# Later sums of weights, carries ahead of weight copies, and last-layer output tiles by ScalarE copy and accumulating DMA, in a two-layer hybrid trunk

## The chip, the cores and the metric

The kernel runs on one core of one Trainium2 chip. The metric is the device time of one execution in microseconds (us). A core has TensorE (PE, matrix products), VectorE (DVE), ScalarE (ACT), GpSimd (POOL) and SyncE (SP). In this kernel SP does nothing but issue DMAs, and POOL and ACT issue some too. All matrix products land in PSUM and have to be evacuated from there by DVE or ACT.

## The reference, cut to what matters

The model is a trunk of two layers over 16 meta tokens and 512 tokens, 1024 channels, float32.

```
for l in range(DEPTH):                                   # DEPTH = 2
    h = rmsnorm(h_res, norm_gain[l])
    proj = h @ w_in[l]
    u_pool, z_pool, c_q, c_kv, k_rope, z_mla, g_pool, g_mla = jnp.split(proj, IN_SPLIT_POINTS, axis=-1)
    y_pool = (pool_mix(u_pool, pool_w_group[l], pool_scale[l]) * silu(z_pool)) @ pool_w_up[l]
    o_mla = mla(c_q, c_kv, k_rope, pos, ...)             # 8 heads, causal attention
    y_mla = (o_mla * silu(z_mla)) @ mla_w_up[l]
    merged = sigmoid(g_pool) * y_pool + sigmoid(g_mla) * y_mla
    h_res = h_res + merged @ w_out[l]
return h_res[:, N_META:]
```

Two places of it matter here: `pool_w_group` (in the kernel `wgr`, the weights of the grouped pooling), and the last line of a layer, the product with `w_out` that is added to the residual stream.

## The kernel before, in words

Everything is kept with channels on the 128 partitions and tokens along the free dimension: the residual stream is `xb`, 8 tiles of 528 tokens (the last layer works on 512). A product in float32 accuracy is made of three faster ones: each operand is split into a high and a low part, and `mm3` issues high by high, low by high and high by low (L192, L195, L196). A weight tile of 128 by 512 goes through four hands: SP loads it into one of three `raw` buffers (L115), ACT copies it to the high part `whi` (L187), DVE subtracts to get the low part `wlo` (L188), and PE uses both.

`register` writes a plan, a list of products in the order in which their weights come: c_kv, c_q, then for m = 0 to 3 a pool product `u`m followed by a key product `k`m, then the values `v`, then `yw` (the load of `wgr`, `held` in two `sv` buffers until the pooling product `y` uses it), and so on to the output products. `stream` walks over the plan, calls the weight load of a product a few products ahead, and advances a clock `clk` by what it has issued. The order of the instructions on each engine is then settled by a scheduler with a simulated timeline, so a small edit can move rows on all engines. `behind(a, b)` ties instruction a behind instruction b; `newest[0]` is the newest matmul at that point, and `earlier(ns)` is the newest matmul that was issued at least so many ns ago by that clock.

The output product. Tiles o0, o1, o2 and o3 are plain products with four rows of weight chunks (evacuated by `ev_o`, L1092: one DVE instruction that adds half of the PSUM bank to `xb`). The other four tiles are made of two pairs u = 0, 1 by a scheme with seven products in place of eight (`out_pairs`): p = 1, 2, 7, 6, 5 between o2 and o3 (called "oa"), and p = 4, 3 after o3 ("ob"). It needs sums of weight tiles (`wsum`), which are made in DRAM during the layer by SP copies and accumulating POOL DMAs (`weight_sums`, L359). Bank "a" of a pair carries a running sum through the products 1, 6, 5 and 3. After p = 1, 6 and 5 its value also has to be added to another part of `xb`: `carry` (L1163) lets ACT copy the bank into an `sv` buffer, and POOL issues a DMA that adds that buffer to `xb` (L1164). The next product into the same bank can't start before the ACT copy has read it. Finished parts of `xb` leave in the last layer by `yT` DMAs (L1101 in `out`, issued by POOL, in "ob" by SP).

A row name such as `p2u1` below is product 2 of pair 1.

Of the kernel before, what the change touches and what calls it, by code (L numbers as in the profile page):

```python
# [10 lines left out]
F32R = mybir.dt.float32r  # L11
BF16 = mybir.dt.bfloat16
I32 = mybir.dt.int32
AF = mybir.ActivationFunctionType
ALU = mybir.AluOpType
# [7 lines left out]
NM = 16  # L23
# [49 lines left out]
def trunk(ctx, tc, xT, pos, win, wkr, wqb, wkb, wvb, wgr, wpu, wmu, wout, gains, const, yT):  # L73
    nc = tc.nc
    pe, act, dve, gp, sp = nc.tensor, nc.scalar, nc.vector, nc.gpsimd, nc.sync
# [11 lines left out]
    def nm(s):  # L87
        uid[0] += 1
        return f"{s}_{uid[0]}"

    def slot(tag, dt=F32, bufs=1, w=W):
        return sl.tile([P, w], dt, tag=tag, name=nm(tag), bufs=bufs)

    def tmp(w=W):
        return tp.tile([P, w], F32, tag="tmp", name=nm("tmp"), bufs=3)
# [18 lines left out]
    def fetch(src, n, raw, eng):  # L114
        eng.dma_start(raw[:, :n], src)  # L115
        return raw

    def rawt():
        return wp.tile([P, 512], F32, tag="raw", name=nm("raw"), bufs=3)
# [49 lines left out]
            return self.src[c // 512] if isinstance(self.src, list) else self.src[:, c:c + n]  # L169

    loads = [0]

    def wload(src, n, gain, spare, buf=None, held=False):
        raw = early.pop(0) if early else fetch(src, n, buf or rawt(), sp)
        loads[0] += 1
        pool, th, tl, nb = (tp, "th", "tl", 2) if loads[0] <= 2 or spare else (wp, "whi", "wlo", 3)
        if gain is not None:
            v = raw[:, :n].rearrange("p (k m) -> p k m", k=8)
            gp.tensor_mul(v, v, gain.unsqueeze(2).to_broadcast([P, 8, n // 8]))
            return raw, None  # L180
        if held:
            hi, lo = slot("sv", F32R, bufs=2), slot("sv", F32R, bufs=2)
            split(hi, lo, raw[:, :n], 0, n)
            return hi, lo
        hi = pool.tile([P, W if pool is tp else 512], F32R, tag=th, name=nm("whi"), bufs=nb)
        lo = pool.tile([P, W if pool is tp else 512], F32R, tag=tl, name=nm("wlo"), bufs=nb)
        act.activation(hi[:, :n], raw[:, :n], AF.Copy)  # L187
        dve.tensor_sub(lo[:, :n], raw[:, :n], hi[:, :n].bitcast(F32))  # L188
        return hi, lo

# [10 lines left out]
    def earlier(ns):  # L201
        return next((m for c, m in reversed(past) if c <= clk[0] - ns), past[0][1])

    newest = [None]
    plan = []
# [96 lines left out]
    def split(hi, lo, src, a, b):  # L302
        act.activation(hi[:, a:b], src, AF.Copy)  # L303
        dve.tensor_sub(lo[:, a:b], src, hi[:, a:b].bitcast(F32))  # L304

    def behind(ins, other):
        tc.add_manual_dep(ins.ins, other.ins.name,
                          mybir.DependencyInfo(mybir.DependencyClass.Sync, mybir.DependencyReason.DATA))
# [38 lines left out]
    def weight_sums(name, w):  # L347
        def made(u, i):
            a, b = w[2 * u], w[2 * u + 1]
            d = wsum[name][u]  # L350
            src = {0: (b[:, 0:512], b[:, 512:1024]), 2: (a[:, 0:512], b[:, 0:512]), 1: (a[:, 0:512], d[:, 0, :]),
                   3: (a[:, 512:1024], d[:, 1, :])}
            return d[:, i, :], src[i]

        def copy(d, src):
            behind(sp.dma_start(d, src[0]), earlier(14000))

        def add(d, src):
            behind(gp.dma_start(d, src[1], accum_op=ALU.add), earlier(4000))  # L359

        for u in range(len(w) // 2):
            for fn, i in ((copy, 0), (copy, 2), (add, 0), (copy, 1), (add, 2), (add, 1), (copy, 3), (add, 3)):
                yield lambda fn=fn, u=u, i=i: fn(*made(u, i))

    class Layer:
# [723 lines left out]
        def ev_o(self, m, nxt):  # L1089
            def ev(ps, a, b):  # L1090
                x = xb[:, m, a:b]
                dve.scalar_tensor_tensor(out=x, in0=ps, scalar=0.5, in1=x, op0=ALU.mult, op1=ALU.add)  # L1092
                self.out(m, (a, b), nxt, gp)
                if not self.last and m == 3 and b == T:
                    nxt.square_x(m)
            return ev
# [46 lines left out]
        def out_pairs(self, nxt, name, products):  # L1143
            order = [(p, u) for p in products for u in range(2)]
            l = self.l
            a, b, c = self.halves()
            n = b - a
            A, B = (a, b), (b, c)
            src = []
            for p, u in order:  # L1150
                w0, w1 = wout[l, OUT[2 * u]], wout[l, OUT[2 * u + 1]]
                src.append({1: w0[:, 0:512], 2: w0[:, 512:1024], 4: w1[:, 512:1024]}.get(p))
                if src[-1] is None:
                    src[-1] = wsum[l][u][:, {5: 0, 6: 1, 7: 2, 3: 3}[p], :]
            bank = self.banks

            def grow(m, s, v):
                x = xb[:, m, s[0]:s[1]]
                dve.scalar_tensor_tensor(out=x, in0=v, scalar=0.5, in1=x, op0=ALU.mult, op1=ALU.add)

            def carry(m, s, v, u, scale, o):
                t = self.carried[u][:, o:o + n]
                act.activation(t, v, AF.Copy, scale=scale)  # L1163
                gp.dma_start(xb[:, m, s[0]:s[1]], t, accum_op=ALU.add)  # L1164

            def body(i, w):
                p, u = order[i]
                m0, m1 = OUT[2 * u:2 * u + 2]
                key = {2: "e", 7: "c", 4: "c"}.get(p, "a"), u
                if key not in bank:  # L1170
                    bank[key] = (sct if key[0] == "a" else mmt)()
                ps = bank[key][:, :n]
                t, o = (B if p == 3 else A), (0 if p == 1 else 4)
                for k in range(4):
                    xh, xl = (x[:, t[0]:t[1]] for x in self.mg[k + o]) if p < 4 else self.tt[k][p]
                    c_ = P * k
                    mm3(ps, w[0][:, c_:c_ + P], w[1][:, c_:c_ + P], xh, xl, k == 0 and p in (1, 2, 7), k == 3, True)
                    if k == 1:
                        yield 6 * (n / 2.4)
                q = sp if name == "ob" else gp  # L1180
                if p == 1:
                    self.carried[u] = slot("sv", bufs=2)
                    carry(m0, A, ps, u, 0.5, 0)
                elif p == 2:
                    grow(m0, A, ps)
                    self.out(m0, A, nxt, q)
                elif p == 7:
                    grow(m1, B, ps)
                elif p == 6:
                    carry(m1, A, ps, u, -0.5, HALF)  # L1190
                elif p == 5:
                    carry(m1, B, ps, u, -0.5, 0)
                    self.out(m1, B, nxt, q)
                    if u == 1 and not self.last:
                        for m in range(3):
                            nxt.square_x(m)
                elif p == 4:
                    grow(m1, A, ps)
                    self.out(m1, A, nxt, q)
                else:  # L1200
                    grow(m0, B, ps)
                    self.out(m0, B, nxt, q)
                    if not self.last:
                        nxt.square_x(m0)
                        nxt.square_x(m1)
                if i == len(order) - 1:
                    done.add((l, name))
                yield 6 * (n / 2.4)

            plan.append(Gemm((l, name), src, 512 * len(src), body=body))  # L1210
            plan[-1].more = True

        def register(self, nxt):
            l, XS = self.l, self.XS
# [3 lines left out]
            def add(name, src, width, **kw):  # L1218
                plan.append(Gemm((l, name), src, width, **kw))
# [8 lines left out]
            def kk(p):  # L1228
                add(f"k{p}", wkb[l, p], 256, evac=self.ev_k(p), xs=cs, segs=FULL)
# [2 lines left out]
                cq(m)  # L1232
            for m in range(4):
                add(f"u{m}", wi(MT_U + m), D, evac=self.ev_u(m), xs=hs, segs=FULL)
                if m == 1:
                    add("kr", wkr[l], 256, body=self.kr_body, gain=gn[:, l * N_GAIN + G_H:l * N_GAIN + G_H + 8])
                kk(m)
# [4 lines left out]
                add(f"y{m}", None, P, body=self.y_body(m))  # L1242

            add("v", wvb[l], 1024, body=self.v_body)
            add("yw", wgr[l], 512, body=self.hold)
            plan[-1].held = True
            zp(0)
            zp(1)
            y(0)
# [15 lines left out]
            if self.last:  # L1265
                for e in ("gm0", "gm1", "gp0", "gm2", "gp1", "gm3", "gp2", "gm4", "gp3", "gm5", "gm6", "gm7"):
                    m = int(e[2])
# [10 lines left out]
                add(f"mu{m}", wmu[l, m], 512, evac=self.ev_mu(m), xs=lambda: self.ogs, segs=XS)  # L1278
                plan[-1].spare = m % 2 == 1
            mg = lambda: self.mg  # L1280
            self.banks, self.carried = {}, {}
            for m in range(4):
                if m == 3:
                    self.out_pairs(nxt, "oa", (1, 2, 7, 6, 5))
# [165 lines left out]
```

## Time and profile before

| | |
|---|---|
| time, median of 3 runs | 781.85 us (781.79 to 782.32) |
| the profiled execution, its own time | 781.9 us |
| its span in the trace | 780.1 us |
| granted TensorE clock | 1.00 |
| busy in the span: PE, DVE, ACT, POOL | 773.2, 569.7, 444.7, 232.7 us |
| matmuls in the trace | 5469 |
| DMA, mean over the span | 145 GB/s |

The page of the profile lists busy times by engine, the chain of work that ended last and groups of instructions by line. The timeline of one engine lists its instructions in a stretch, with the idle time before each in brackets and the instruction that ended it. Matmuls are pipelined: a row's duration (0.28 us for 256 or 264 columns) is longer than the distance between the starts of two of them (0.12 us), so a wait of PE is read as the distance between two starts less the usual distance.

### The profile page before, as it was taken

How to read it: one execution, taken by the hardware profiler on the slowest of the kernel's cores; microseconds unless marked ns; L12 is line 12 of the kernel's file. 1: busy time of each engine (PE TensorE's matmuls, PEld its weight loads, DVE VectorE, ACT ScalarE, POOL GpSimd, SP SyncE). 2: the span in 40 equal slices, each digit the busy share in tenths (PEclk: the TensorE clock that was granted, in tenths of full speed). 3: DMA queues.
4: the chain of work that ended last, by engine and by line, in shares of the span. 5: the costliest groups of instructions: out<-in, count | busy, mean ns of one | idle time of the engine just before them, and what ended most of it. 6: DMA issues, size and time to landing. Idle time of an engine off the chain costs nothing.

```text
span 780.1 us, 15325 instructions
## 1 busy us (share of the span) xinstructions
PE 773.2 (99%) x5469; PEld 710.9 (91%) x5469; DVE 569.7 (73%) x1326; ACT 444.7 (57%) x1016; POOL 232.7 (30%) x303
## 2 busy tenths in 40 slices
PE   9999999999999999999999999999999999999998
PEld 8999899999999999999997898887788999988887
DVE  5848787446778876589764577866897888864994
ACT  7645555645566665645564446546657766664552
POOL 1024525103335333211330136221006625340213
PEclk9999999999999999999999999999999999999999
DMA  6232457765646465565662424425557666662645
GB/s 245 82 96 89 125 171 151 177 168 144 156 110 164 116 141 120 156 156 184 169 171 82 109 75 122 133 62 178 146 132 167 173 187 158 175 226 72 210 137 154
DMA packets 65325, 112.92 MB, mean 145 GB/s; under 512 B 10704, under 2 KB 15696, under 8 KB 65248
## 3 DMA queue, kind: packets, MB, share of 16 engines
q1 hardware_dynamic: 55344, 92.18, 39.1%
q0 software_dynamic: 8896, 17.92, 12.9%
q10 hardware_dynamic: 1008, 1.84, 0.7%
q8 instruction: 43, 0.70, 0.4%
q14 instruction: 34, 0.28, 0.1%
HBM read 100.18 MB, written 22.62 MB: 157 GB/s over the span
## 4 chain that ended last, share of the span: by engine, by line
PE 91%; DVE 4%; DMA 2%; ACT 1%; issue 1%; POOL 0%; DVEq 0%; ACTq 0%; POOLq 0%
PE mm L192 26%; PE mm L196 26%; PE mm L195 25%; PE S L195 3%; PE S L196 3%; PE S L192 3%; PE mm L979 2%; DVE wlo L188 1%; PE o L985 1%; PE o L984 1%; PE S L506 1%; DMA raw<-wgr 1%; DMA xb<-xT 1%; PE mm L408 1%; ACT whi L187 0%
## 5 line engine op out<-in xcount | busy, mean ns | idle before, releaser
L192 PE MATMUL mm<-hh,whi 128*128 128x264 f32 (+2 forms) x992 | 306.2, 311 | 0.5 <-DVE u L550 0.4
L196 PE MATMUL mm<-hh,wlo 128*128 128x264 f32 (+2 forms) x992 | 304.4, 309 | 0.1
L195 PE MATMUL mm<-hl,whi 128*128 128x264 f32 (+2 forms) x992 | 304.1, 308 | 0.0
L188 DVE TENSOR_TENSOR wlo<-raw,whi 128x512 fp32r<-128x512 f32 (+1 forms) x253 | 180.0, 714 | 100.3 <-ACT whi L187 98.0
L187 ACT ACTIVATE whi<-raw 128x512 fp32r<-128x512 f32 (+1 forms) x253 | 154.2, 613 | 168.7 <-PE mm L195 110.2
L192 PEld LDWEIGHTS mm<-hh,whi 128*128 128x128 f32 x992 | 186.2, 188 | 11.3 <-issue 1.0
L195 PEld LDWEIGHTS mm<-hl,whi 128*128 128x128 f32 x992 | 186.8, 188 | 8.7
L196 PEld LDWEIGHTS mm<-hh,wlo 128*128 128x128 f32 x992 | 185.9, 188 | 9.0 <-DVE wlo L188 0.6
L922 POOL TENSOR_SCALAR pa<-pa,rs 128x272 f32<-128x272 f32 (+1 forms) x32 | 33.2, 1038 | 103.3 <-DVE rs L941 64.5
L922 POOL TENSOR_SCALAR cq<-cq,rs 128x400 f32<-128x400 f32 (+1 forms) x32 | 51.2, 1600 | 0.0
L192 PE MATMUL mm<-cq,whi 128*128 128x264 f32 (+2 forms) x140 | 43.8, 313 | 0.0
L195 PE MATMUL mm<-cq,whi 128*128 128x264 f32 (+2 forms) x140 | 43.7, 312 | 0.0
L196 PE MATMUL mm<-cq,wlo 128*128 128x264 f32 (+2 forms) x140 | 43.3, 312 | 0.1
L908 DVE CUSTOM_DVE_ANT_0 S<-S,maskw,nqs 128x272 f32<-128x272 f32 (+4 forms) x80 | 38.6, 498 | 5.3 <-PE S L196 5.0
L725 POOL TENSOR_TENSOR racc<-racc,tmp 128x264 f32<-128x264 f32 (+1 forms) x15 | 14.0, 936 | 85.5 <-ACT tmp L724 85.5
L304 DVE TENSOR_TENSOR tl<-mm,th 128x512 fp32r<-128x512 f32 (+1 forms) x64 | 30.0, 483 | 8.0 <-ACT th L303 6.3
L359 POOL DMA_DIRECT2D wsum<-wout x8 | 7.0, 875 | 91.6 <-PE mm L196 86.9
L303 ACT ACTIVATE th<-mm 128x512 fp32r<-128x512 f32 (+1 forms) x64 | 26.3, 433 | 10.2 <-PE mm L979 9.6
L915 ACT ACTIVATE cq<-S,bia 128x400 f32<-128x400 f32 (+2 forms) x48 | 24.5, 514 | 13.2 <-DVE bia L953 8.5
L192 PE MATMUL mm<-u,whi 128*128 128x264 f32 (+1 forms) x96 | 31.3, 326 | 0.0
L196 PE MATMUL mm<-u,wlo 128*128 128x264 f32 (+1 forms) x96 | 30.9, 322 | 0.0
L195 PE MATMUL mm<-kn,whi 128*128 128x264 f32 (+1 forms) x96 | 30.6, 320 | 0.0
(344 smaller groups left out, 1684.7 us busy)
## 6 DMA issues: line engine op xcount, KB each, us to landing
raw<-win SPq DMA_DIRECT2D x139, 256.0 KB, 2.8
raw<-wout SPq DMA_DIRECT2D x22, 256.0 KB, 3.6
bc<-kdr SPq DMA_DIRECT2D x16, 264.0 KB, 4.5
wsum<-wout SPq DMA_DIRECT2D x16, 256.0 KB, 3.5
raw<-wpu SPq DMA_DIRECT2D x16, 256.0 KB, 2.7
wsumgp<-win SPq DMA_DIRECT2D x16, 256.0 KB, 3.4
raw<-wmu SPq DMA_DIRECT2D x16, 256.0 KB, 2.8
raw<-wsumgp SPq DMA_DIRECT2D x16, 256.0 KB, 4.3
```

The costliest lines, as they stand in the source:

```text
L187: act.activation(hi[:, :n], raw[:, :n], AF.Copy)
L188: dve.tensor_sub(lo[:, :n], raw[:, :n], hi[:, :n].bitcast(F32))
L192: first = pe.matmul(out, wh, xh, start=start, stop=False, skip_group_check=more)
L195: pe.matmul(out, wh, xl, start=False, stop=False, skip_group_check=more)
L196: newest[0] = pe.matmul(out, wl, xh, start=False, stop=stop, skip_group_check=more)
L303: act.activation(hi[:, a:b], src, AF.Copy)
L304: dve.tensor_sub(lo[:, a:b], src, hi[:, a:b].bitcast(F32))
L725: self.acc_last = gp.tensor_add(self.acc[:, a:b], self.acc[:, a:b], t[:, :b - a])
L908: dve.tensor_tensor_reduce(out=sv, in0=sv, in1=mask, scale=nqs[:, i, h:h + 1], scalar=3e38, op0=ALU.add, op1=ALU.min, accum_out=bia[:, c:c ...
L915: act.activation(pv, sv, AF.Exp, scale=-1.0, bias=bia[:, i:i + 1], accum_out=rs[:, c:c + 1])
L922: gp.tensor_scalar(pt[i], pt[i], rs[:, i:i + 1], None, op0=ALU.mult)
L979: pe.transpose(tr[:, P * (i - j):P * (i - j + 1)], pt[i][:, NM + P * j:NM + P * (j + 1)], ident)
```

## The change

Five edits, in one diff:

1. `add` in `weight_sums`: the accumulating POOL DMAs are tied to a matmul 9000 ns back by the planner's clock where it was 4000.
2. `yw`: the load of `wgr` moves in the plan from behind `v` to behind `u2`; it gets a buffer of its own (tag `bc`, which the kernel otherwise uses later for another purpose) in place of one of the three `raw`, and its DMA is tied behind the newest matmul.
3. `urgent`: of the weight copies that are called for after a carry, the second and the third are tied behind the carry's ACT copy.
4. `ev_o` in the last layer, m = 0, 1, 2: ACT copies half of the bank into `tmp`, and a POOL DMA adds that to `xb`, in place of the DVE instruction.
5. The `yT` DMAs of those three tiles aren't issued by POOL at once, but by SP at the first product of "ob", behind its last matmul.

```diff
+    urgent = []
     def wload(src, n, gain, spare, buf=None, held=False):
+        if held:
+            hi, lo = slot("sv", F32R, bufs=2), slot("sv", F32R, bufs=2)
+            raw = slot("bc", bufs=3)
+            behind(sp.dma_start(raw[:, :n], src), newest[0])
+            split(hi, lo, raw[:, :n], 0, n)
+            return hi, lo
         raw = early.pop(0) if early else fetch(src, n, buf or rawt(), sp)
...
-        if held:
-            hi, lo = slot("sv", F32R, bufs=2), slot("sv", F32R, bufs=2)
-            split(hi, lo, raw[:, :n], 0, n)
-            return hi, lo
...
-        act.activation(hi[:, :n], raw[:, :n], AF.Copy)
+        made = act.activation(hi[:, :n], raw[:, :n], AF.Copy)
+        for e in urgent:
+            e[1] += 1
+            if 1 < e[1] < 4:
+                behind(made, e[0])
...
         def add(d, src):
-            behind(gp.dma_start(d, src[1], accum_op=ALU.add), earlier(4000))
+            behind(gp.dma_start(d, src[1], accum_op=ALU.add), earlier(9000))
...
             def ev(ps, a, b):
                 x = xb[:, m, a:b]
+                if self.last and m < 3:
+                    t = tmp()[:, a:b]
+                    act.activation(t, ps, AF.Copy, scale=0.5)
+                    gp.dma_start(x, t, accum_op=ALU.add)
+                    self.later.append(lambda: behind(sp.dma_start(yT[:, m, a - NM:b - NM], x), newest[0]))
+                    return
...
             def carry(m, s, v, u, scale, o):
                 t = self.carried[u][:, o:o + n]
-                act.activation(t, v, AF.Copy, scale=scale)
+                urgent.append([act.activation(t, v, AF.Copy, scale=scale), 0])
                 gp.dma_start(xb[:, m, s[0]:s[1]], t, accum_op=ALU.add)
...
+                while self.later and name == "ob":
+                    self.later.pop(0)()
...
                 add(f"u{m}", wi(MT_U + m), D, evac=self.ev_u(m), xs=hs, segs=FULL)
+                if m == 2:
+                    add("yw", wgr[l], 512, body=self.hold)
+                    plan[-1].held = True
...
             add("v", wvb[l], 1024, body=self.v_body)
-            add("yw", wgr[l], 512, body=self.hold)
-            plan[-1].held = True
```

In the changed kernel the lines lie lower: L187 is L190, L188 is L195, L303 and L304 are L310 and L311, L396 is L403, L550 is L557, L1163 is L1176, and the new ACT copy of `ev_o` is L1101.

What this does to the order of instructions is shown at three places. The first is ACT in the last layer, where the products 1 of both pairs end. `whi` rows are weight copies, `sv` rows the two carries, `sq` and `rinv` rows the splitting of other operands. Before:

```order
907 L187 ACTIVATE whi_10084<-raw_10082 128x512
908 L303 ACTIVATE sq_9831<-cq_1871_9599 128x256
909 L187 ACTIVATE whi_10105<-kh_10103 128x512
910 L187 ACTIVATE whi_10145<-kl_10143 128x512
911 L303 ACTIVATE sq_9835<-cq_1872_9601 128x256
912 L303 ACTIVATE sq_9839<-cq_1856_9557 128x256
913 L187 ACTIVATE whi_10125<-raw_10123 128x512
914 L1163 ACTIVATE sv_10036<-S_10023 128x256
915 L1163 ACTIVATE sv_10058<-S_10045 128x256
916 L303 ACTIVATE rinv_9843<-cq_1876_9627 128x256
```

The same place now:

```order
907 L310 ACTIVATE sq_9835<-cq_1872_9601 128x256
908 L310 ACTIVATE sq_9839<-cq_1856_9557 128x256
909 L1101 ACTIVATE tmp_10017<-mm_9974 128x512
910 L310 ACTIVATE rinv_9843<-cq_1876_9627 128x256
911 L1176 ACTIVATE sv_10039<-S_10026 128x256
912 L1176 ACTIVATE sv_10061<-S_10048 128x256
913 L190 ACTIVATE whi_10066<-kl_10064 128x512
914 L190 ACTIVATE whi_10087<-raw_10085 128x512
915 L190 ACTIVATE whi_10108<-kh_10106 128x512
916 L190 ACTIVATE whi_10128<-raw_10126 128x512
```

The weight copies of p7u0, p7u1, p6u1 and p6u0 stood directly ahead of the two carries, and that of p2u1 (`whi_10063`) still further up, at row 885. Now those of p2u1, p7u0, p7u1 and p6u0 (`whi_10066` to `whi_10128`; the numbers are counted anew) all stand behind them.

The second place is ACT where the same products of the first layer end. The three L396 rows (L403 now) square `xb` for the next layer's norm. Before:

```order
461 L187 ACTIVATE whi_5549<-kh_5547 128x512
462 L396 ACTIVATE cq_1005_5669<-xb 128x528
463 L396 ACTIVATE cq_1006_5671<-xb 128x528
464 L187 ACTIVATE whi_5569<-raw_5567 128x512
465 L1163 ACTIVATE sv_5480<-S_5467 128x264
466 L1163 ACTIVATE sv_5502<-S_5489 128x264
467 L396 ACTIVATE cq_1007_5673<-xb 128x528
468 L187 ACTIVATE whi_5609<-raw_5607 128x512
469 L187 ACTIVATE whi_5589<-kl_5587 128x512
```

The same place now:

```order
458 L403 ACTIVATE cq_1005_5669<-xb 128x528
459 L403 ACTIVATE cq_1006_5671<-xb 128x528
460 L403 ACTIVATE cq_1007_5673<-xb 128x528
461 L1176 ACTIVATE sv_5480<-S_5467 128x264
462 L1176 ACTIVATE sv_5502<-S_5489 128x264
463 L190 ACTIVATE whi_5507<-kl_5505 128x512
464 L190 ACTIVATE whi_5528<-raw_5526 128x512
465 L190 ACTIVATE whi_5549<-kh_5547 128x512
466 L190 ACTIVATE whi_5569<-raw_5567 128x512
```

`whi_5507` (p2u1) was row 437 before, and `whi_5528` (p7u0) was row 459; both stand behind the two carries now.

The third place is DVE in the first layer around the split of `wgr` (`sv` by L304, L311 now) and the two evacuations of u3 (the last two L550 rows, L557 now). Before:

```order
113 L539 STREAM_SHUFFLE tmp_1040<-kn_164_975 128x264
114 L188 TENSOR_TENSOR wlo_1175<-raw_1172,whi_1174 128x256
115 L540 TENSOR_TENSOR tmp_1040<-tmp_1040,ts_104 128x264
116 L188 TENSOR_TENSOR wlo_1215<-raw_1212,whi_1214 128x512
117 L550 TENSOR_TENSOR u_206_1190<-mm_1146,rinv_480 128x264
118 L304 TENSOR_TENSOR sv_1258<-raw_1255,sv_1257 128x512
119 L550 TENSOR_TENSOR u_206_1190<-mm_1147,rinv_480 128x264
```

The same place now:

```order
113 L311 TENSOR_TENSOR sv_1078<-bc_1079,sv_1077 128x512
114 L546 STREAM_SHUFFLE tmp_1040<-kn_164_975 128x264
115 L195 TENSOR_TENSOR wlo_1181<-raw_1178,whi_1180 128x256
116 L547 TENSOR_TENSOR tmp_1040<-tmp_1040,ts_104 128x264
117 L195 TENSOR_TENSOR wlo_1221<-raw_1218,whi_1220 128x512
118 L557 TENSOR_TENSOR u_209_1196<-mm_1152,rinv_480 128x264
119 L557 TENSOR_TENSOR u_209_1196<-mm_1153,rinv_480 128x264
```

The split of `wgr` went from between the two evacuations to a place five rows ahead of the first. On SP its load went from behind the two loads of `wvb` to ahead of them.

2 lines of the change are left out of this document (1 added, 1 removed).

## The prediction

> **What bounds the kernel now.** I read the page first: busy times and the chain that ended last.
>
> ```profile
> PE 773.2 (99%) x5469; PEld 710.9 (91%) x5469; DVE 569.7 (73%) x1326; ACT 444.7 (57%) x1016; POOL 232.7 (30%) x303
> PE 91%; DVE 4%; DMA 2%; ACT 1%; issue 1%; POOL 0%; DVEq 0%; ACTq 0%; POOLq 0%
> ```
>
> PE is busy in 99% of the span, and the change takes no product away. So it can only win the moments in which PE waits, and the table of PE's waits says how few those are.
>
> ```profile
> PE S L192 <- ACT sv L1163: 1.1, 1, 1.1
> PE mm L192 <- DVE u L550: 0.8, 2, 0.4
> ```
>
> The first is one wait for a carry, the second two waits for the evacuation of u3, one in each layer. Their price is the distance of two starts. First u3 in layer 0, then in layer 1 (timeline of PE):
>
> ```profile
> 83.58 0.40 PE L196 MATMUL mm<-whi,kl 128*128 128x512 f32 x1
> 84.38 0.50 PE L192 MATMUL mm<-whi,kh 128*128 128x512 f32 x1 [0.41 <-DVE u L550]
> 84.72 0.39 PE L195 MATMUL mm<-wlo,kh 128*128 128x512 f32 x1
> 84.95 0.39 PE L196 MATMUL mm<-whi,kl 128*128 128x512 f32 x1
> ```
> ```profile
> 476.03 0.40 PE L196 MATMUL mm<-whi,kl 128*128 128x512 f32 x1
> 476.48 0.50 PE L192 MATMUL mm<-whi,kh 128*128 128x512 f32 x1
> ```
>
> A 512-column matmul starts 0.23 us after the last (84.72 to 84.95). So layer 0 lost 0.80 - 0.23 = 0.57 us, layer 1 lost 0.45 - 0.23 = 0.22. After each wait the next start is also about 0.1 late (84.38 to 84.72 is 0.34); I leave that out for waits lost and waits made alike. Now the carry in the last layer, PE and then ACT:
>
> ```profile
> 755.73 0.28 PE L196 MATMUL mm<-hh,wlo 128*128 128x256 f32 x1
> 757.08 0.39 PE L192 MATMUL S<-cq,whi 128*128 128x256 f32 x1 [1.07 <-ACT sv L1163]
> ```
> ```profile
> 756.12 0.63 ACT L187 ACTIVATE whi<-raw 128x512 fp32r<-128x512 f32 x1 [1.57 <-PE mm L196]
> 756.66 0.64 ACT L1163 ACTIVATE sv<-S 128x256 f32<-128x256 f32 x2
> ```
>
> That is 1.35 - 0.12 = 1.23 us. A weight copy that waited for PE to free its buffer stood on ACT ahead of the carry that PE needed. All that the change can win is 0.57 + 0.22 + 1.23 = 2.02 us, 0.26% of 781.9. The rest of the span is PE in an even step, and ahead of it a start-up that the change leaves alone.
>
> **The early load of `wgr`.** Why u3 was late (chain of waits, layer 0):
>
> ```profile
> 79.42 2.87 DMA raw<-wgr
> 82.32 0.64 ACT sv L303
> 82.98 0.04 DVE sv L304
> ...
> 83.91 0.43 DVE u L550
> ```
>
> The load could start only when a `raw` buffer came free, at 79.42. DVE stood still for its split, between the two evacuations of u3. Now the load is tied to a matmul in the middle of u2. From 68.40, where u2 starts, 36 of its 48 matmuls at 0.121 us end near 73.0. With the same 2.87 us it lands at 75.9, and with ACT's 0.64 its high part is there at 76.6, when DVE reaches its new place only at 78.4, behind the key product's evacuation.
>
> ```profile
> 68.40 0.36 PE L192 MATMUL mm<-hh,whi 128*128 128x264 f32 x1
> 78.08 0.42 DVE L749 TENSOR_TENSOR kn<-mm,q 128x264 f32<-128x264 f32 x1
> 80.22 1.57 DVE L188 TENSOR_TENSOR wlo<-raw,whi 128x512 fp32r<-128x512 f32 x1
> 81.72 0.42 DVE L550 TENSOR_TENSOR u<-mm,rinv 128x264 f32<-128x264 f32 x1
> ```
>
> The split puts 0.6 us ahead of what stands there. The first evacuation goes from 81.72 to 82.3, the second follows at 82.7 and is over at 83.1. PE wants the banks at 83.1 and 83.8, so the whole 0.57 goes, and 0.22 in layer 1, where the order is the same. I take 0.79 won, with 0 as the other end: DVE's instructions here vary (the `wlo` at 80.22 took 1.57), and 0.5 more would give the wait back. On ACT the new copy holds up the key norms behind it until about 76.6; their first user on DVE stands behind the split, at 79.0, which covers it. On SP the load now stands ahead of both `wvb` loads, so these wait for 73.0 too; they need `raw` buffers that DVE frees with `wlo` rows later than that, so I price it at 0.
>
> **The later sums.** POOL's longest wait in sum stands in front of these DMAs:
>
> ```profile
> POOL wsum L359 <- PE mm L196: 107.6, 11, 46.9
> ```
>
> An older matmul shortens these waits and moves POOL's pooled-mean work by a row or two. Nothing in PE's waits names POOL. I take 0, from -0.1 to 0.1: sums come so early that even a wait of 46.9 on POOL held nobody up. If that cover were gone, the price would be a late weight load, as the 0.57 above.
>
> **The carries go first, layer 0.** Here PE had no wait. ACT, then PE:
>
> ```profile
> 377.47 1.16 ACT L396 ACTIVATE cq<-xb 128x528 f32<-128x528 f32 x2
> 378.75 0.63 ACT L187 ACTIVATE whi<-raw 128x512 fp32r<-128x512 f32 x1
> 379.29 0.65 ACT L1163 ACTIVATE sv<-S 128x264 f32<-128x264 f32 x2
> 379.83 0.65 ACT L396 ACTIVATE cq<-xb 128x528 f32<-128x528 f32 x1
> ...
> 381.12 0.62 ACT L187 ACTIVATE whi<-kl 128x512 fp32r<-128x512 f32 x1
> ```
> ```profile
> 378.56 0.28 PE L196 MATMUL S<-hh,wlo 128*128 128x264 f32 x1
> 378.68 0.28 PE L192 MATMUL mm<-hh,whi 128*128 128x264 f32 x1
> ```
>
> The copy for p2u1 was made long before; in the new order it stands behind both carries. Count from the start of the last matmul of p1u0. It ends 0.28 us later; both carries take ACT 0.54 (379.29 to 379.83), the copy 0.63, and handing over some 0.05 twice: p2u1 can start after 1.55 us. PE fills this with the ten products left of p2u0, so it asks after 11 steps of 0.12, 1.32: a wait of 0.2 to 0.35. Then it has two products (0.24) until it asks for the copy of p7u0, which comes 0.53 after the first: another 0.3. From there ACT makes a copy each 0.53, PE uses one in 1.45, and no copy is late. Sum 0.6. If the three squares in front end late (they wait for DVE's part of `xb`), it is more.
>
> DVE adds something here. Its first add of a finished product waits until the carry's DMA has landed:
>
> ```profile
> 380.10 1.80 POOL L1164 DMA_DIRECT2D xb<-sv  x2 [1.36 <-ACT sv L1163]
> 384.83 0.43 DVE L1159 SCALAR_TENSOR_TENSOR xb<-mm,xb 128x264 f32<-128x264 f32 x1 [1.50 <-DMA xb<-sv]
> 385.18 0.68 DVE L188 TENSOR_TENSOR wlo<-raw,whi 128x512 fp32r<-128x512 f32 x1
> ```
>
> Before, 4.7 us lay between issue and add, and the needed `wlo` stood ahead of it. In the new order the `wlo` of p6u0 stands behind that add. With the carry 0.7 earlier the DMA goes out near 379.4, the add comes at 384.1 and the `wlo` is there at 385.1, when PE asks at 385. I add 0.1. Layer 0 costs 0.7, from 0.3 to 1.6 (the DMA 1 us later).
>
> **The carries go first, last layer.** The same count gives 0.6, and here p1u0's own copy comes with it: by ACT's new order it is there some 0.2 after PE wants it. I take 0.75, from 0.3 to 1.5. DVE has room here: 14.85 of 15 us were busy before, and three adds of 0.60 to 0.68 go away.
>
> ```profile
> 754.82 0.68 DVE L1092 SCALAR_TENSOR_TENSOR xb<-mm,xb 128x512 f32<-128x512 f32 x1
> 745.00:760.00 15.00, 13.93 (x96) 12.74 (x96) 14.85 (x36) 9.27 (x22) 3.53 (x5) 1.00 0.44 131
> 770.00:780.10 10.10, 6.91 (x53) 6.44 (x51) 2.86 (x6) 0.02 (x1) 2.60 (x4) 1.00 0.39 118
> ```
>
> (Columns after the stretch: its length, busy PE, PE's weight loads, DVE, ACT, POOL, then clock, DMA share, GB/s.) ACT, 9.27 busy of 15, gets three copies of about 0.6 instead; none stands in front of a carry that is ready, since o2's ends with the product that PE has just left.
>
> **The three output tiles.** Their `yT` DMAs, 3 x 256 KB, left from POOL after each DVE add (the last began at 754.82); now SP issues them behind the last matmul of p4u0, which lies 34 starts of 0.118 us before the last matmul, near 772.6.
>
> ```profile
> 776.63 0.28 PE L196 MATMUL S<-hh,wlo 128*128 128x256 f32 x1
> 776.95 0.42 DVE L1159 SCALAR_TENSOR_TENSOR xb<-S,xb 128x256 f32<-128x256 f32 x1 [0.97 <-PE S L196]
> yT<-xb SPq DMA_DIRECT2D x4, 128.0 KB, 2.3
> ```
>
> From 770 on the engines moved 118 GB/s at a share of 0.39, which makes 302 GB/s at full share. 786 KB more are 2.6 us of all 16 engines, beside the 3.9 (0.39 x 10.1) of before. Between 773 and 779.7 there is room for 6.5 us in all, and 1 us of the old 3.9 lies before 773: the room is just enough, but the last small transfer stands behind them on SP's queue. I take 0.3 late, from 0 to 1.2. The Trainium skill, DMA: Bandwidth & Descriptors, section Issuing engines are not separate DMA queues, says that DMAs of all issuers end on the same 16 engines and interleave, so that another issuer saves only issue time. By its Specifications (some 27 GiB/s for each engine) the 786 KB would be 1.7 us, and the end would not move; the row above is slower, and the sum goes by the row.
>
> **How the numbers follow.** -0.57 - 0.22 - 1.23 + 0.7 + 0.75 + 0.3 = -0.27. From 781.9 (span 780.1 and 1.8 around it, which stays; the median is 781.85) that is 781.6. About 0.2%, 1.6 us, is what a measurement can tell from no change. Forecast, chance 0.44: 781.6, within that bound.
>
> **Rivals.** (1) The copies come in time, because the scheduler's order leaves more slack than my count: the three waits go and nothing replaces them but the ends' 0 to 0.4: 780.0 (781.9 - 2.0 + 0.1). For it: a handover of 0.05 less here and there takes a third of each new wait away. Against: four copies stand behind the carries where none did. Chance 0.22, faster.
> (2) The copies behind the carries cost both layers their upper bounds: the first layer 1.6 (squares late, the `wlo` behind the landed carry), the last 1.5, and 0.5 at the end: 781.9 - 2.0 + 3.6 = 783.5, slower. It decides from 3.6 us of new waits on, that is when the `wlo` of p6u0 comes 1 us after PE asks. For it: 4.7 us from issue to add. Chance 0.15.
> (3) The end is bound by DMA: none of the 2.6 us finds room, with the two output queues sharing engines: 781.9 - 2.02 + 1.45 + 2.6 = 783.9, slower. Against: the share of 0.39 before. Chance 0.09.
> (4) The early load doesn't do what it should, because DVE is late anyway at u3: 0.79 stays, 782.4, within the bound. Chance 0.10.
>
> Faster 0.22, same 0.44 + 0.10 = 0.54, slower 0.24. The range 780.0 to 783.6 takes in the forecast, (4), most of (1) and of (2); (3) and the far ends are left out, under 0.2.
>
> **What would show it.** In the profile after, PE's waits should no longer name DVE u at 84 and 476, nor 1.1 us for a carry; in their place a wait or two of 0.2 to 0.4 for ACT's `whi` near 380 and near 755, with `whi` directly behind `sv` on ACT. The three 256 KB `yT` should leave SP near 772, and the last small `yT` should land no more than 0.3 us later after its issue than the 2.3 of before. Wrong would be: no `whi` waits at all (1), a wait for `wlo` near 385 of 1 us (2), or PE ending before 776 with a span that does not follow (3).

## The result and the profile after

The changed kernel takes 786.36 us (median of 7 runs, 783.76 to 791.67), the kernel before 782.32 us in the same series (7 runs, 781.72 to 783.95). The ratio is 1.0053, with a 95% interval of 1.0038 to 1.0067: slower by 0.5%. The forecast was 781.6, in a range of 780.0 to 783.6, so it was wrong in sign and in size. The profiled execution of after took 785.74 us with a span of 783.6; that is 3.5 us more span than before's 780.1. Both traced executions are on the short side: before's 781.9 against medians of 782.3 to 783.3 in this series and those below, after's 785.7 against 786.4.

The page of after, busy times and the shares of the chain that ended last:

```profile
PE 775.4 (99%) x5469; PEld 712.7 (91%) x5469; DVE 569.9 (73%) x1323; ACT 446.1 (57%) x1019; POOL 230.3 (29%) x303
PE 89%; DVE 4%; issue 3%; DMA 2%; ACT 1%; POOL 1%; SPq 0%; DVEq 0%; ACTq 0%; POOLq 0%
```

PE has the same 5469 matmuls. DVE has three instructions fewer and ACT three more, which is the move of the three output tiles. In the waits of PE in after, the columns are the sum in us, the count and the longest:

```profile
PE S L199 <- ACT kh L310: 1.2, 1, 1.2
PE wps L137 <- DVE na L849: 1.0, 1, 1.0
PE mm L199 <- ACT q L310: 0.9, 1, 0.9
PE S L203 <- DVE wlo L195: 0.7, 1, 0.7
PE mm L199 <- DVE u L557: 0.2, 1, 0.2
```

The 1.1 us for the carry's `sv` is gone, and so are both waits for u3 (the 0.2 for `u` stands at 59.6, ahead of every edit). The 1.0 at the first matmul is the start-up. Three new single waits stand in the table, each about as long as the carry wait that went. I take them in order of time.

**The wait at 334, for a weight load.** The chain of waits around it, first before, then after (start, length, what):

```profile
328.35 2.55 DMA raw<-wmu
...
330.98 0.64 ACT whi L187
...
333.90 0.21 ACT q L303
```
```profile
329.00 3.41 DMA raw<-wmu
...
332.49 0.64 ACT whi L190
...
335.41 0.21 ACT q L310
...
335.66 0.39 PE mm L199
```

From the landing on, the two chains are alike: high part on ACT, low part and the `mo`/`cq` steps on DVE, `q` on ACT, then PE. What differs is the load itself: 3.41 - 2.55 = 0.86 us. PE had its last product before the wait at 334.45 and starts again at 335.66, so it lost 1.21 - 0.12 = 1.09; before, the same place (333.80 to 334.15) lost 0.23. The difference is 0.86 again. What other DMAs were out at that time is on POOL's timeline, first before, then after:

```profile
329.27 0.81 POOL L359 DMA_DIRECT2D wsumgp<-win  x1 [8.68 <-PE mm L196]
330.14 0.83 POOL L359 DMA_DIRECT2D wsumgp<-wsumgp  x1
```
```profile
325.05 0.81 POOL L366 DMA_DIRECT2D wsumgp<-win  x1 [8.03 <-PE mm L203]
325.61 1.11 POOL L366 DMA_DIRECT2D wsumgp<-wsumgp  x1
```

These are the accumulating DMAs of the sums of weights, tied to an older matmul by the change. They left at 329.3, beside a load that had begun at 328.4; now they leave at 325.1 and 325.6, some 4 us ahead of the load at 329.0. The engines' share shows it (windows, the same 5 us of before and after; DMA share and GB/s are the last two columns):

```profile
325.00:330.00 5.00, 5.00 (x42) 5.00 (x42) 3.69 (x10) 4.29 (x15) 0.73 (x1) 1.00 0.29 69
325.00:330.00 5.00, 5.00 (x41) 4.83 (x41) 3.50 (x9) 3.88 (x14) 1.68 (x2) 1.00 0.75 109
```

**The wait at 668, for another load.** The chain of after, POOL's timeline, and PE before at the same place:

```profile
663.14 4.29 DMA raw<-win
...
667.54 0.63 ACT whi L190
668.17 0.54 ACT kh L310
...
668.76 0.39 PE S L199
```
```profile
660.80 0.88 POOL L366 DMA_DIRECT2D wsum<-wsum  x1 [1.05 <-PE mm L203]
```
```profile
665.59 0.39 PE L195 MATMUL mm<-hl,whi 128*128 128x512 f32 x1
665.89 0.71 PE L192 MATMUL S<-kh,qhl 128*128 128x272 f32 x3
```

ACT made the copy of this weight ahead of `kh`, in the order of before too, so the scores of the attention waited for a load that they don't use. PE stood from 667.20 to 668.76, 1.33 us more than a step of 0.23; before, it was 0.07. A sum's DMA, which went out at 652.97 and 666.09 before, now goes out at 660.80, 2.3 us ahead of the load.

**The wait at 764, in the last layer.** DVE, POOL and PE of after:

```profile
757.00 0.86 POOL L1177 DMA_DIRECT2D xb<-sv  x1
```
```profile
762.90 0.42 DVE L1172 SCALAR_TENSOR_TENSOR xb<-mm,xb 128x256 f32<-128x256 f32 x1 [1.88 <-DMA xb<-sv]
763.24 0.68 DVE L195 TENSOR_TENSOR wlo<-raw,whi 128x512 fp32r<-128x512 f32 x1
```
```profile
763.61 0.28 PE L202 MATMUL S<-u,whi 128*128 128x256 f32 x1
764.58 0.39 PE L203 MATMUL S<-cq,wlo 128*128 128x256 f32 x1 [0.68 <-DVE wlo L195]
```

A `wlo` that PE needs stands on DVE behind an add that waits for the carry's DMA; issue to add is 5.9 us. PE loses 0.97 - 0.12 = 0.85.

**The sum.** Matching the matmuls of the two traces in their order gives where the span's 3.5 us came from. The product u2 starts at 69.20 instead of 68.40: 0.80 late before any edit acts; in the fourteen kernels this point lies anywhere from 67.4 to 69.6, so I put it down to chance. Then -0.45 and -0.29 at u3 in the two layers, +0.6 at the carries of layer 0, +0.86 at 334, +1.3 at 668, +0.35 for the whole tail (the lost carry wait against the new ones), and the end: the last add starts 3.15 us ahead of the end before and 3.50 after, +0.35. Together 3.5. Smaller differences at other places cancel: +0.3 near 140, +0.3 near 450, -0.5 between 640 and 664 and -0.1 behind that.

### The profile page after: what moved, and what is told of

Same layout as the page of the kernel before. It is cut to its first block, busy times and chain, and to the rows that moved or that the text cites. A ratio compares the mean times of both kernels' runs of the same rounds, so it can differ in the third digit from the quotient of the medians.

```text
span 783.6 us, 15318 instructions
## 1 busy us (share of the span) xinstructions
PE 775.4 (99%) x5469; PEld 712.7 (91%) x5469; DVE 569.9 (73%) x1323; ACT 446.1 (57%) x1019; POOL 230.3 (29%) x303
## 4 chain that ended last, share of the span: by engine, by line
PE 89%; DVE 4%; issue 3%; DMA 2%; ACT 1%; POOL 1%; SPq 0%; DVEq 0%; ACTq 0%; POOLq 0%
PE mm L199 25%; PE mm L203 25%; PE mm L202 24%; PE S L203 2%; PE S L199 2%; PE S L202 2%; PE mm L986 2%; DVE wlo L195 2%; PE o L992 1%; PE o L991 1%; PE S L513 1%; DMA xb<-sv 1%; PE mm L415 1%; ACT whi L190 1%; DMA raw<-win 1%
## 5 line engine op out<-in xcount | busy, mean ns | idle before, releaser
L195 DVE TENSOR_TENSOR wlo<-raw,whi 128x512 fp32r<-128x512 f32 (+1 forms) x253 | 181.1, 719 | 106.1 <-ACT whi L190 104.0
L190 ACT ACTIVATE whi<-raw 128x512 fp32r<-128x512 f32 (+1 forms) x253 | 154.1, 613 | 163.7 <-PE mm L202 97.6
L929 POOL TENSOR_SCALAR pa<-pa,rs 128x272 f32<-128x272 f32 (+1 forms) x32 | 30.5, 954 | 85.0 <-DVE rs L948 42.4
L929 POOL TENSOR_SCALAR cq<-cq,rs 128x400 f32<-128x400 f32 (+1 forms) x32 | 52.8, 1651 | 0.0
L311 DVE TENSOR_TENSOR tl<-mm,th 128x512 fp32r<-128x512 f32 (+1 forms) x64 | 30.0, 483 | 7.8 <-ACT th L310 6.1
L310 ACT ACTIVATE th<-mm 128x512 fp32r<-128x512 f32 (+1 forms) x64 | 26.2, 433 | 9.8 <-PE mm L986 8.7
L199 PE MATMUL mm<-q,whi 128*128 128x264 f32 (+1 forms) x96 | 29.8, 322 | 0.9 <-ACT q L310 0.9
```

The source lines that it names most:

```text
L190: made = act.activation(hi[:, :n], raw[:, :n], AF.Copy)
L199: first = pe.matmul(out, wh, xh, start=start, stop=False, skip_group_check=more)
L929: gp.tensor_scalar(pt[i], pt[i], rs[:, i:i + 1], None, op0=ALU.mult)
```

## The experiments

There were two theories. The first: the sums' later DMAs delay weight loads that PE is about to need, and this makes the change a loss. The rival is the prediction's own rival 2: ordering the carries ahead of the weight copies costs more than counted, and the sums are innocent. A third question was which edit removes the carry wait. Of five edits I call them: the sums' tie (1), the early load of `wgr` (2), the ties of the carries (3), and the three output tiles with their late DMAs (4 and 5).

**Edit 1 undone in after.**

```diff
-            behind(gp.dma_start(d, src[1], accum_op=ALU.add), earlier(9000))
+            behind(gp.dma_start(d, src[1], accum_op=ALU.add), earlier(4000))
```

> The changed kernel with its first edit undone (accumulating DMAs of the sums tied 4000 ns back again). Theory A, that the moved sum DMAs run into weight loads: the two waits that are new in the attention of both layers (PE for ACT q near 335, 0.9 us, and for ACT kh near 668, 1.2 us) go, and the span falls by 1.5 to 2.5 us against the changed kernel's 783.6. Rival B, that these two waits are only loads which landed late by chance in that execution: they come and go without regard to this edit, and the median stays within 0.7 us of the changed kernel's 786.4.

784.35 us, ratio to before 1.0019 (1.0007 to 1.0032). About two thirds of the loss go (0.53% to 0.19%). The wait at 334 falls to 0.39, the one at 668 is gone, and the tail's 0.8 stays.

**Edit 1 alone in before** (the same line, the other way).

> The kernel before with the first edit alone. Theory A: the waits near 335 (0.8 us or more beyond the 0.23 of before) and near 668 (1.2 us) appear, nothing else changes: 1.8 to 2.5 us slower than the kernel before, ratio 1.002 to 1.003. Rival: they needed the other edits too, and the ratio lies within 0.001 of 1.

786.15 us, ratio 1.0036 (1.0023 to 1.0049). The one number makes waits of 1.27 at 334 and 1.12 at 667. That is what I expected of the trace (2.1 us more than before at the two places); the time grew by 2.9 us, more than the 1.8 to 2.5 expected, and where the rest goes is open. The sums are not innocent.

**The sums' DMAs made small in after.** The order of instructions stays; the accumulating DMAs add 64 of 512 columns, so the rest of the sums is left out.

```diff
-            behind(gp.dma_start(d, src[1], accum_op=ALU.add), earlier(9000))
+            behind(gp.dma_start(d[:, 0:64], src[1][:, 0:64], accum_op=ALU.add), earlier(9000))
```

> The changed kernel with the accumulating DMAs of the sums cut to an eighth of their columns (64 of 512); every instruction stays in its place, and the sums of the other columns are left out. Theory A in its sharp form, traffic of these DMAs slows the weight loads beside them: the waits near 335 and 668 fall to 0.4 us or less, 1.5 to 2.2 us faster than the changed kernel. Rival, that it is POOL's place in the order (the descriptors or POOL's own work, not the bytes) that makes the loads late: both waits stay over 0.7 us.

782.68 us, ratio 0.9991 (0.9982 to 0.9999), where after had 1.0053: 0.6% less, which is more than the 1.5 to 2.2 us expected. Of the 3.5 us between the two traces, 2.0 lie at the two waits, 0.8 in the start-up and the rest at places that vary from one execution to the next. The two loads of above, from this kernel's chain:

```profile
327.80 2.73 DMA raw<-wmu
```
```profile
661.03 3.04 DMA raw<-win
```

2.73 instead of 3.41, and 3.04 instead of 4.29. The waits behind them are 0.41 and 0.23. POOL issues the two DMAs ahead of the first load exactly as before this edit: 3.95 and 3.39 us ahead of it, in 0.81 and 1.11 us of its time. So with the order of all instructions unchanged, the bytes of the sums decide: this is contention among DMAs, not a wait of POOL. Whether it is in the DMA engines themselves or in the memory behind them, these runs don't separate. The price of one and the same lead also varies: in the three other traces with 9000 and full sums the first load took 3.60, 3.62 and 4.93 us, the second 3.97, 4.46 and 4.04.

**Edit 3 undone in after.**

```diff
-            if 1 < e[1] < 4:
+            if False:
```

> The changed kernel with its third edit undone (weight copies not tied behind carries). By theory A the new small waits near 381 and 757 (0.4 us each) go, a wait for the carry of about 1.2 us near 756 comes back, and the sum moves by less than 0.7 us. By the rival, that the third edit costs most of the loss, it is faster than the changed kernel by 1.5 us or more.

783.68 us, ratio 1.0020 (1.0005 to 1.0034). The waits of the sums remain (1.30 and 1.29), the wait at 380 and all waits in the tail go. So the rival's condition is met as well (2.7 us less than after in the medians, where 1.5 was asked): edits 1 and 3 each cost. My expectation was wrong in one thing that matters: the carry wait of 1.23 did not come back. DVE in the tail of this kernel:

```profile
761.37 0.42 DVE L1172 SCALAR_TENSOR_TENSOR xb<-mm,xb 128x256 f32<-128x256 f32 x1
761.71 0.68 DVE L195 TENSOR_TENSOR wlo<-raw,whi 128x512 fp32r<-128x512 f32 x1
```

Without the ties the weight copies stand ahead on ACT, so their `wlo` rows are made ahead of the adds, and nothing that PE needs stands behind the carry's landing.

**Edit 3 alone in before.**

> The kernel before with the third edit alone. The prediction's count: the carry's 1.23 us goes and 0.6 to 0.75 us of waits for weight copies comes in each layer, so within 0.3 us of the kernel before. What the profile after suggests: 0.4 us in the first layer, 0.4 near 756 and 0.5 to 0.8 near 762 for a low part behind an add that waits for the carry's DMA: 0.1 us faster to 0.5 slower. Rival: over 1 us slower, with a wait at the tail of more than 1.5 us.

785.05 us, ratio 1.0026 (1.0014 to 1.0037). Against my expectation (0.1 faster to 0.5 slower) this is the rival's case, 1.8 us slower. Layer 0 has lost 0.6 us; the tail's waits sum to 2.3 us against 1.23 before. No wait for a carry's `sv` is left among them: the ties too remove it. But 0.9 of the 2.3 is a wait for a load of `wsum` that took 5.91 us, and the `wlo` behind the carry's landing, which I expected, costs nothing here. The ties lose in both layers.

**Edits 4 and 5 undone in after** (the three tiles evacuated by DVE again).

```diff
-                if self.last and m < 3:
+                if False:
```

> The changed kernel with its fourth and fifth edit undone (DVE adds the three last-layer tiles, POOL issues their output at once). Theory A, that the three accumulating DMAs delay the carry's own one on POOL's queue: the wait of 0.7 to 0.85 us for a low part near 764 goes, since the carry's DMA is issued near 755 and not 757 and lands in about 4 us and not 5.8; the end moves by 0.8 to 1.5 us. Rival B, that the low part is late because its place on DVE is behind the add by the third edit's order: the wait stays, at 0.5 us or more. The two attention waits stay by both.

787.18 us, ratio 1.0064 (1.0050 to 1.0078): no better than after. So edits 4 and 5 are not the loss. Of the two theories the second has it: a wait of 0.53 for a low part stays, at 766, but the add ahead of that `wlo` waits for its product and not for the carry's DMA. This run also showed the clock, below, which is part of its time.

**Edits 4 and 5 alone in before, and edit 2 alone.**

> The kernel before with the fourth and fifth edit alone (ScalarE copies with accumulating DMAs for three output tiles, their output late). Theory: these edits, and not the ties, remove the carry's wait of 1.23 us, and no wait over 0.3 us is left from 745 on; the end, from the last add to the end of the span, grows from 3.15 to 3.5 to 3.9 us; the waits for u3 (0.57 and 0.22) stay. So 0.5 to 1.0 us faster than the kernel before. Rival: the carry's wait goes only together with the early load, and the time is the same or longer by up to 0.7 us.

> The kernel before with the second edit alone (early load of the pooled weights in its own buffer). Theory: both waits for the evacuation of u3 go, 0.57 and 0.22 us, nothing else changes, so 0.6 to 0.9 us faster than the kernel before, about 781.1. Rival: the earlier ACT and DVE work makes another instruction late and the gain is under 0.3 us.

782.72 us, ratio 0.9999 (0.9986 to 1.0012), and 783.06 us, ratio 0.9999 (0.9987 to 1.0011). In the trace the first has no carry wait and no tail wait above 0.2, and ends with 3.82 us behind the start of the last add, where before had 3.15. What removed the carry wait is seen on PE and ACT of this kernel:

```profile
755.90 0.28 PE L201 MATMUL S<-hh,wlo 128*128 128x256 f32 x1
758.62 0.28 PE L197 MATMUL S<-cq,whi 128*128 128x256 f32 x1
```
```profile
757.11 0.64 ACT L1174 ACTIVATE sv<-S 128x256 f32<-128x256 f32 x2
```

The first row is the last matmul of the products 1, the second the first one that needs a carried bank. Between them PE now has 22 matmuls, where before had 10 and then the wait: the scheduler has moved 12 of a later product (`mm<-sq`) ahead, so PE asks 1.4 us later. The carries also start sooner, 1.2 us behind the first row, where it was 2.1 before; a weight copy still stands directly ahead of them on ACT.

The second has lost both u3 waits (-0.46 and -0.29) and kept a carry wait of 1.58. Neither shows in the time: both steps are under 1 us, and waits of 0 to 1.3 us at 57 and 450, at places that no edit touches, differ from one profiled execution to the next. Before's traced execution had none of the wait at 450. I had expected 0.5 to 1.0 us from the first and 0.6 to 0.9 from the second; as times these two are inconclusive.

**Edits 2, 4 and 5 together in before**, that is after without the sums' tie and the carries' ties.

> The kernel before with the second, fourth and fifth edit (early load of the pooled weights; ScalarE copies and accumulating DMAs for three output tiles, their output late); sums at 4000 ns and no weight copy tied to a carry. Theory A (the first edit makes the two attention waits, the third edit makes the waits of the tail, the others win): no wait over 0.4 us at 335, 668 and from 745 on, the carry's wait of 1.23 us gone: 1.5 to 2.0 us faster than the kernel before, ratio 0.9975 to 0.9985. Rival (the early load's gain is eaten elsewhere, the late output costs at the end): within 0.7 us of the kernel before.

781.37 us against 783.28 for before in that series, ratio 0.9978 (0.9965 to 0.9991). This is faster than both kernels, and as expected. The head of PE's waits of this kernel:

```profile
PE wps L137 <- DVE na L849: 1.0, 1, 1.0
PE mm L986 <- POOL pa L929: 0.4, 1, 0.4
```

Behind the start-up no wait in this table is longer than that 0.4. The three ratios of the parts multiply to 1.0036 x 1.0026 x 0.9978 = 1.0040, just inside after's interval (1.0038 to 1.0067): the parts can explain the whole, though each is known to some 0.0013 only and the ties cost more beside the new output path (below).

**The carry's DMAs made small**, with edit 1 undone, so that only the tail is looked at. They add 32 of 256 columns; the rest of the carried sums is left out.

```diff
-                gp.dma_start(xb[:, m, s[0]:s[1]], t, accum_op=ALU.add)
+                gp.dma_start(xb[:, m, s[0]:s[0] + 32], t[:, 0:32], accum_op=ALU.add)
```

> The changed kernel with sums at 4000 ns, as the first experiment, and the carries' accumulating DMAs cut to 32 of their 256 columns (the rest of what they add is left out); the order moves by two rows. Theory: in the tail PE waits 0.8 us near 761 for a low part that stands on DVE behind an add, and the add waits for the carry's DMA, which took 5.8 us from issue to landing; with an eighth of the bytes it lands in 2 to 3.5 us, the wait falls to 0.2 or less and the tail gets 0.6 us shorter or more. Rival: the DMA's fixed part and the place in POOL's queue make up those 5.8 us, the wait stays over 0.5 us.

783.40 us, ratio 1.0003 (0.9993 to 1.0013). DVE in the tail:

```profile
760.08 0.42 DVE L1172 SCALAR_TENSOR_TENSOR xb<-mm,xb 128x256 f32<-128x256 f32 x1 [2.34 <-PE mm L203]
760.42 1.28 DVE L195 TENSOR_TENSOR wlo<-raw,whi 128x512 fp32r<-128x512 f32 x2
```

The add now waits for its product, not for the DMA, and PE's wait of 0.81 at 761 (in the kernel with edit 1 undone) falls to 0.18. The landing of the carry was what the `wlo` stood behind.

**The sums tied nearer still**, in the version with edits 2, 4 and 5.

```diff
-            behind(gp.dma_start(d, src[1], accum_op=ALU.add), earlier(4000))
+            behind(gp.dma_start(d, src[1], accum_op=ALU.add), earlier(2000))
```

> The fifth experiment with the sums' accumulating DMAs tied 2000 ns back. If the older tie is bad in itself, a younger one is no worse: within 0.5 us of the fifth experiment, waits near 335 and 668 of 0.4 us or less. If what counts is only which weight loads the DMAs fall on, another wait of over 0.5 us may appear elsewhere, and the time is then 0.5 to 2 us longer.

783.83 us, ratio 1.0015 (1.0001 to 1.0029): slower than with 4000. Its chain and its POOL around 334:

```profile
328.98 5.27 DMA raw<-wmu
```
```profile
325.93 0.88 POOL L366 DMA_DIRECT2D wsumgp<-win  x1 [9.79 <-PE mm L1039]
332.44 0.81 POOL L366 DMA_DIRECT2D wsumgp<-win  x1 [5.63 <-PE mm L203]
333.37 0.83 POOL L366 DMA_DIRECT2D wsumgp<-wsumgp  x1
```

So it isn't that older is worse. 9000 and 2000 both put a sum's DMA some 3 to 4 us ahead of this load, and 4000 happens to put none there. What counts is which load the DMA runs into. The load took 5.27 us with one such DMA ahead of it and two more issued while it ran; I didn't separate the shares of the three.

**The outputs sent earlier**, in the version with edits 2, 4 and 5: SP sends the three tiles after the product pairs named "oa".

```diff
-                while self.later and name == "ob":
+                while self.later and i == len(order) - 1:
```

> The fifth experiment (early load, ScalarE copies, no ties, sums at 4000 ns) with the three late outputs issued by SP at the end of the first group of pair products, near 765, in place of the first product of the last group, near 772. Theory: the end, from the last add to the end of the span, is 3.9 us there and 3.15 us before the change, because three outputs of 256 KB share the engines with the last ones; it falls to 3.2 or less, and the time by 0.4 to 0.8 us against the fifth experiment: ratio to the kernel before 0.997. Rival: the outputs now run into the last weight loads, and a wait for a weight copy of 0.3 us or more takes the gain.

781.79 us, ratio 0.9982 (0.9971 to 0.9992). From the start of the last add to the end it is 3.48 us against 3.88, but the time, expected at 0.997, can't be told from the 0.9978 of above. No gain is shown.

## Why the prediction was wrong

**What bounds the kernel** held: PE stays 99% busy, and single waits of PE decide. Of the 3.5 us between the two traces, all but the 0.35 at the end was found in the starts of PE's matmuls, 0.8 of it as chance ahead of the edits.

**The early load** held. Predicted -0.57 and -0.22; PE's time shows -0.45 and -0.29. All ten kernels that have the early load pass the first place some 0.5 us sooner behind u2, and the three changed ones that lack it don't. In after, PE goes from the first bank of u3 to the second without a gap:

```profile
84.57 0.40 PE L203 MATMUL mm<-whi,kl 128*128 128x512 f32 x1
84.81 0.39 PE L199 MATMUL mm<-whi,kh 128*128 128x512 f32 x1
```

**The later sums** is the step that failed. "Nothing in PE's waits names POOL. I take 0, from -0.1 to 0.1." I asked who waits for POOL. I should have asked what POOL's DMAs share with the loads that PE waits for. They cost 0.86 + 1.3 = 2.2 us in the trace of after, and 0.36% (2.8 us) alone. The prediction did name the form of the price, "a late weight load", for the case that the cover of the sums were gone; the cover for the sums was there, and it was the other loads that came late. I had the rule in hand, and used it at the end of the kernel only: the Trainium skill, DMA: Bandwidth & Descriptors, section Issuing engines are not separate DMA queues, says that DMAs of all issuers run on the same 16 engines and interleave. The 2.73 against 3.41 us of one load agrees. The page of before could not have given the price, but the trace could have shown the risk: a wait of 0.23 at 334 means that this load had no slack at all.

**The carry wait** of 1.23 went, but the ties (3), which were credited with it, weren't needed for that. Either of the two removes it: it is gone with the ties alone (edit 3 alone, and edits 4 and 5 undone), and gone with the output tiles (4 and 5) in all five kernels that have them without the ties, which are 1.44 to 1.5 us shorter in the tail. Only with neither does it stay, at 1.58 (edit 2 alone) and 1.10 (edit 1 alone). So beside the output tiles the ties had nothing left to win and kept their price. That the tiles would move PE's own order was not in the prediction; that part is luck.

**The carries go first, layer 0:** predicted 0.7, measured 0.6 in every kernel that has the ties. The count of ACT's copies was nearly right: the two waits for `whi` at 381 are 0.23 and 0.17 by the prediction's measure, where it had 0.2 to 0.35 and 0.3, and the slower start behind each makes the rest of the 0.6. The 0.1 for a `wlo` near 385 did not come.

**The carries go first, last layer:** predicted 0.75 with DVE given room, so that with the carry wait gone the tail should have been 0.48 us shorter; it was 0.35 longer. This is the second step that failed. Beside the new output path the ties cost 1.8 us in the tail (from -1.45 to +0.35); without it a net 0.8 to 1.2 remains after the carry wait that they remove. The wait for p1u0's own copy came too (0.25 at 750, where 0.2 was counted). The `whi` waits near 757 came as said, since ACT now makes both carries ahead of three copies:

```profile
756.19 0.66 ACT L1176 ACTIVATE sv<-S 128x256 f32<-128x256 f32 x2 [0.28 <-PE S L203]
756.74 0.63 ACT L190 ACTIVATE whi<-kl 128x512 fp32r<-128x512 f32 x1
```

What I left out is the `wlo` behind the add. I had found just this step in layer 0, priced it at 0.1 there, and then looked only at DVE's busy time in the last layer. There the carry's DMA goes out 1 us behind the last one of the output tiles (POOL issued that at 756.03) and takes 5.8 us from issue to landing. That the tiles' DMAs make it so long is not shown: with edits 4 and 5 undone the two carries there took 3.1 and 5.6 us.

**The end** held: +0.35 against 0.3 predicted (range 0 to 1.2). The three large DMAs cost it no more than that, so rival 3's 2.6 us did not come. They left near 776, which is the 772.6 of the prediction on a trace that runs 3.15 us late by then, with the small ones behind them on SP:

```profile
776.09 0.85 SPq L1103 DMA_DIRECT2D yT<-xb  x2
...
778.27 2.61 SPq L1114 DMA_DIRECT2D yT<-xb  x3
```

Of the **rivals**, 2 had the right sign and one right part, the `wlo` behind the landed carry, though it named layer 0 and it came in the last layer. None named the sums, which were the largest term. After's remaining distance, 4.0 us in the medians against 2.7 that the terms give without the late start, is not settled in full: three of after's seven runs (786.36, 788.45 and 791.67) had a mean granted clock of 0.997 instead of 1.000, which fits the clock below, but there is no trace of such a run of after.

## What to carry to other kernels

A DMA that nobody waits for still has a price: look up which loads start in the 4 us behind it, and how much slack the consumer of each has; a consumer that already waits 0.2 us has none. A tie that moves one instruction forward on an engine moves others behind it, so follow each of those to its users on the next engine, here from ACT's copy to DVE's `wlo` to the add that waits for a DMA. And credit a vanished wait to an edit only after a run of that edit alone and one of the others without it: here two edits each removed the same wait, and one of them was a loss.

## What the runs showed of the hardware

A long wait of PE cost a second time in two of the kernels. With edits 4 and 5 undone, the load of the wait at 334 took 4.93 us (from 326.88 on), and PE stood still:

```profile
332.33 0.28 PE L203 MATMUL mm<-hh,wlo 128*128 128x264 f32 x1
335.06 0.51 PE L199 MATMUL mm<-q,whi 128*128 128x264 f32 x2 [2.45 <-ACT q L310]
```

The windows of the same kernel (the third number from the right is the granted clock):

```profile
335.00:336.00 1.00, 0.94 (x6) 0.94 (x7) 1.00 (x5) 0.87 (x4) 0.00 (x0) 0.75 1.04 397
336.00:337.00 1.00, 1.00 (x6) 1.00 (x6) 1.00 (x4) 0.82 (x3) 0.00 (x0) 0.50 0.05 18
...
338.00:339.00 1.00, 1.00 (x7) 1.00 (x6) 0.00 (x0) 0.00 (x0) 0.00 (x0) 0.54 0.81 164
```

Some 0.5 us after PE resumed, the clock was halved for 3.4 us: matmuls started 0.22 us apart instead of 0.12, which cost about another 1.5 us. The same followed an idle time of 2.78 us in the kernel with the sums at 2000. After idle times of 0.9 to 1.2 us the clock stayed at 1.00. The Trainium skill, TensorE: Matmul & The Clock Gate, Part 1: The HAM clock gate, gives an idle window of about 3.4 us as what brings the half clock; here 2.45 us were enough, so the measurement decides. In these kernels it makes a late weight load a cliff, not a slope: of the kernel with the sums at 2000, ten of twelve runs had a mean clock of 0.998 or less.
